# Token-layout projections of a hybrid token mixer: blocks of 512 weight columns instead of 256, with another split of the PSUM banks

## The chip, the cores and the metric

The kernel runs on one core of one Trainium2 chip. The metric is the device time of one execution in microseconds (us). The profiler's trace of one execution is read beside it. Five engines work side by side, each through its own list of instructions and strictly in that list's order: TensorE (PE, with PEld for its weight loads), VectorE (DVE), ScalarE (ACT), GpSimd (POOL) and SyncE (SP), which issues the transfers.

## The reference

Two layers work on 512 tokens: 256 context tokens and 256 latent ones, four tiles of 128 (t = 0, 1 context; t = 2, 3 latent). The width is 1024.

```
h = rms_norm(x) * (1 + scale) + shift             # scale, shift, gate from c @ w_mod
p = [h @ w for w in split(w_in)]                  # all input projections, 13872 columns
y_a = rms_norm((ssd_scan forward + backward + d*x) * silu(z))            # 16 heads of 64
s   = softmax(q k^T) for two maps of 64 dims per head                    # 8 heads
y_b = rms_norm((s_0 - lam * s_1) @ v) * silu(dz)
y_c = rms_norm((mlstm forward + backward) * sigmoid(o)) * silu(z)        # 4 heads, d_v = 256
x   = x + gate * ((sum_b sigmoid(g_b) * (y_b @ w_branch_b)) @ w_out)
```

Context tokens attend only to context, latent tokens to both. Everything is float32; the output is the latent stream after the second layer. In the second layer the context tokens are projected only where the latent ones read them (k, v, the scan inputs).

## The kernel before

**Products.** Every float32 operand of a projection is split into a high and a low part, so a product takes three matmuls per 128 rows of depth: high by high, high by low, low by high. The tokens' parts are `hh` and `hl`, the weights' parts `whi` and `wlo`.

**Weights.** They come in pieces of 128 x 1024 floats ("granules", L122ff): SP starts a transfer into `raw`, ACT casts it to `whi` (L119), DVE subtracts to get `wlo` (L82). Each of the three has three buffers.

**Two kinds of projection.** `proj_ch` (L166ff, matmuls L179 to L181) gives channels on the partitions; its moving operand is 512 tokens wide. `proj_tok` with `mm_tok` (L137 to L164, matmuls L148 to L150) gives tokens on the partitions: the token chunk is stationary, and the weights move, 256 columns at a time. Two token tiles (a "pair") share one PSUM bank, 256 columns each. q, k, v, the gates and the output projection go this way.

**PSUM.** There are eight banks, dealt out in L31 as `ACC, PE_, PM = 3, 3, 2`: three for the sums of projections (`acc`), and five for the mixers in two rotating sets (`pe`, `pm`).

**Order.** The code marks work with three bands: 0 for loads, splits and emptying of banks, 1 for the mixers, 2 for projection matmuls. A scheduler at build time puts each engine's instructions in one fixed order, with the lower band first where its operands are ready by its own model. The projections of later stages are written between the mixers' steps, so that projection matmuls stand between the mixers' matmuls on PE.

**Attention** (L899ff). For each head and query tile, the scores of the two maps go into two `pe` tiles (L917). A map has 64 dimensions; map 0 lies on partitions 0 to 63, map 1 on 64 to 127. Each map takes three matmuls, and the code writes them alternately, map 0, map 1, three times. DVE takes the row maximum (L919), ACT the exponential with its row sum (L921), DVE combines the maps in `E` (L79), PE transposes (L931, into `pe`), ACT copies (`aT`, L933), and PE multiplies with v (L935). All query tiles of a head share one `pm` bank, which ACT empties once a head (L938, L940).

**mLSTM** (L1039ff). For a head and direction, the chunks are gone through in order. In a step PE makes three products (L1067, L1072, L1088); DVE adds the state's part to the numerator (`nu`, L79), renews the state (`C`, L79), divides, and makes `kw` for the next step. The gate projections of a head (`mo_proj`, `mz_proj`) are written ahead of a `ml_core`, their use behind it.

Of the kernel before, what the change touches and what calls it, by code (L numbers as in the profile page):

```python
# [21 lines left out]
NT = 4  # L22
# [8 lines left out]
ACC, PE_, PM = 3, 3, 2  # L31
# [3 lines left out]
def hybrid_backbone_kernel(ctx: ExitStack, tc: tile.TileContext, A, out, dbg=None):  # L35
# [86 lines left out]
    def granules(srcs):  # L122

        for g in range(2):
            with band(0):
                raw = mk(wts, [P, 4, 256], "raw", bufs=3)
                c = 0
                for src in srcs:
                    n = src.shape[1]
                    nc.sync.dma_start(  # L130
                        raw[:, :, c : c + n],
                        src[g * 512 : (g + 1) * 512, :].rearrange("(k p) n -> p k n", p=P),
                    )
                    c += n
                hi = mk(wts, [P, 4, 256], "whi", F32R, bufs=3)
                lo = mk(wts, [P, 4, 256], "wlo", F32R, bufs=3)
                split(raw, hi, lo)  # L137
            yield 4 * g, hi, lo
# [12 lines left out]

    def proj_tok(srcs, lhs, pairs, evac):

        ps = {}
        with band(2):
            for p in pairs:
                ps[p] = pacc()
        for k0, hi, lo in granules(srcs):
            with band(2):
                for p in pairs:  # L160
                    mm_tok(ps[p], lhs, p * 256, k0, hi, lo)
        for p in pairs:
            with band(0):
                evac(p, ps[p].rearrange("p (t n) -> p t n", t=2))  # L164
# [37 lines left out]
    def rsqrt(src, n, scale, eps, pp=P, pool_=True):  # L202
# [6 lines left out]
        xh = mk(small, [P, 32], "rs_x", bufs=2)[:pp, :n]  # L209
        it = mk(small, [P, 32], "rs_i", I32, bufs=2)[:pp, :n]  # L210
        y = mk(small, [P, 32], "rs_y", bufs=3)[:pp, :n]
        a = mk(small, [P, 32], "rs_a", bufs=2)[:pp, :n]
# [237 lines left out]
    for l in range(depth):  # L450
# [228 lines left out]
        def silu2(ps):  # L679
            th = mk(ev, [P, 2, 256], "th", bufs=3)  # L680
            S.activation(th, ps, AF.Tanh, scale=0.5)
            zz = mk(ev, [P, 2, 256], "zz", bufs=2)
            stt(zz, th, 1.0, ps, ALU.add, ALU.mult)
            return zz

# [30 lines left out]
        ssA = mk(small, [P, NT, 4], "ssA", bufs=1)  # L716
# [76 lines left out]
        def z_proj(b):  # L793
            def f(p, ps):
                zz = silu2(ps)
                with band(1):
                    y = ya(b, p)
                    tt(y, y, zz, ALU.mult)
                    sq = mk(ev, [P, 2, 256], "sq", bufs=2)
                    for i in range(2):  # L800
                        S.activation(sq[:, i, :], y[:, i, :], AF.Square, accum_out=ssA[:, 2 * p + i, b : b + 1])

            proj_tok([wcol(O_Z + 256 * b)], hT, pq, f)


        qkv = {}

        def qkv_proj(qt, parts="qkv"):
            if qt not in qkv:
                ssq = mk(small, [P, 2, NT, 4], "ssq", bufs=3)  # L810
                qkv[qt] = {}, ssq
                with band(0):
                    if last:
                        V.memset(ssq, 64.0)
            res, ssq = qkv[qt]
            for nm_ in parts:
                n = "qkv".index(nm_)
                dst = res[nm_] = mk(p8, [P, NT, 256], "p8", bufs=6)

                def f(p, ps, dst=dst, n=n):  # L820
                    o = dst[:, 2 * p : 2 * p + 2, :]
                    S.copy(o, ps)
                    if n < 2:
                        sq = mk(ev, [P, 2, 256], "sq", bufs=2)
                        S.activation(sq, ps, AF.Square)
                        V.tensor_reduce(out=ssq[:, n, 2 * p : 2 * p + 2, :], in_=sq.rearrange("p t (m e) -> p t m e", e=64), axis=AX.X, op=ALU.add)

                proj_tok([wcol((O_Q, O_K, O_V)[n] + 256 * qt)], hT, pq if n == 0 else (0, 1), f)
# [6 lines left out]
        qkv_proj(0)  # L835
# [5 lines left out]
        qkv_proj(1)  # L841
        z_proj(0)
        z_proj(1)
        z_proj(2)
        z_proj(3)
# [12 lines left out]
        def attn_prep(qt):  # L858
            res, ssq = qkv[qt]
            with band(1):  # L860
                rq = rsqrt(ssq.rearrange("p n t m -> p (n t m)"), 32, 1.0 / 64, EPS).rearrange("p (n t m) -> p n t m", n=2, m=4)
                for n, nm_ in enumerate(("q", "k")):
                    for p in pq if n == 0 else (0, 1):
                        ts_ = slice(2 * p, 2 * p + 2)
                        x2 = res[nm_][:, ts_, :]
                        x4 = x2.rearrange("p t (m e) -> p (t m) e", e=64)
                        tt(x4, x4, bc(rq[:, n, ts_, :].rearrange("p t m -> p (t m)"), 64), ALU.mult)
                        if p == 0:
                            tt(x4, x4, gctx[:, n, :].unsqueeze(1).to_broadcast([P, 8, 64]), ALU.mult, eng=G)
                        else:  # L870
# [5 lines left out]
                            x5 = x2.rearrange("p t (m e) -> p t m e", e=64)  # L876
# [6 lines left out]
        def attn_tr(qt, h):  # L883

            res = qkv[qt][0]
            with band(1):
                out = []
                for nm_, ts, f0 in (("q", tq, lo_), ("k", range(NT), 0)):
                    pt = pm()
                    for t in ts:  # L890
                        T.transpose(chunk(pt, t), res[nm_][:, t, h * P : (h + 1) * P], ident)
# [7 lines left out]
        def attn_head(qt, h):  # L899
            vt = qkv[qt][0]["v"]  # L900
            ssB, r0B = aS[qt]
            qh, ql, kh, kl = aS[qt, h]
            with band(1):
                po = pm()
                for t in tq:
# [23 lines left out]
                    pt = pe()  # L929
# [6 lines left out]
                p3 = po.rearrange("p (t e) -> p t e", e=P)  # L936
                for p in pq:
                    S.copy(yb(qt, p)[:, :, h * P : (h + 1) * P], p3[:, 2 * p : 2 * p + 2, :])  # L938
                sq = mk(ap, [P, 512], "rt", bufs=1)
                S.activation(sq[:, lo_:], po[:, lo_:], AF.Square)  # L940
                V.tensor_reduce(out=ssB[:, q_, h], in_=sq[:, lo_:].rearrange("p (t e) -> p t e", e=P), axis=AX.X, op=ALU.add)
# [12 lines left out]
        def dz_proj(b):  # L954
            def f(p, ps):
                zz = silu2(ps)
                with band(1):
                    y = yb(b, p)
                    for i in range(2):
                        for h in range(2):  # L960
                            yy = y[:, i, h * P : (h + 1) * P]
                            stt(yy, yy, riB[b][:, 2 * p + i, h : h + 1], zz[:, i, h * P : (h + 1) * P], ALU.mult, ALU.mult)

            proj_tok([wcol(O_DZ + 256 * b)], hT, pq, f)
# [405 lines left out]
```

## Time and profile before

| | us |
|---|---|
| median of 3 runs | 1708.58 (1705.42 to 1710.35) |
| the profiled execution | 1711.2 |
| its span, first to last instruction | 1709.1 |
| PE busy | 1677.3 |
| DVE busy | 1115.3 |
| ACT busy | 762.7 |
| POOL busy | 164.0 |

The busy time of PE is that of matmuls whose ends overlap; what a matmul costs is read from the distance between the starts of two that follow each other. Of the time outside of PE's busy time most lies at the start. The mean granted clock of TensorE is 0.992 of full speed.

### The profile page before, as it was taken

To read this page: it belongs to the slowest core of one execution; us is meant where nothing else is said; L and a number is where in the kernel's file an instruction comes from. 1 tells how busy PE (TensorE), PEld (TensorE's weight loads), DVE (VectorE), ACT (ScalarE), POOL (GpSimd) and SP (SyncE) were. 2 spreads that over 40 slices of the span, in tenths; PEclk is the share of its full clock that TensorE was granted. 3 is DMA by queue.
4 is the path that set the end of the run, shared out by engine and by line. 5 is a ranking of instruction groups with operands and counts; after the bars stand their busy time and mean duration, and the time that the engine had idled before them with its cause. 6 is when DMAs were issued, how large, how long until landed. Compare 5 with 4: busy or idle time off the path is not lost.

```text
span 1709.1 us, 28774 instructions
## 1 busy us (share of the span) xinstructions
PE 1677.3 (98%) x11448; PEld 1489.2 (87%) x11448; DVE 1115.3 (65%) x2183; ACT 762.7 (45%) x1501; POOL 164.0 (10%) x192
## 2 busy tenths in 40 slices
PE   5999999999999999999999999999999999999998
PEld 2787889999899999977777789988999999999998
DVE  4698887667865666623334354898877867765565
ACT  3455644554544444422223233455555555444453
POOL 0102422101100000000010002012121100000100
PEclk8999999999999999999999999999999999999999
DMA  8522122222222222353544442322242324335654
GB/s 262 128 75 62 50 63 65 73 75 63 76 63 75 64 73 64 125 178 96 182 136 131 163 129 51 108 67 75 79 131 71 101 66 130 93 111 173 179 170 146
DMA packets 191906, 180.38 MB, mean 106 GB/s; under 512 B 20606, under 2 KB 177920, under 8 KB 191772
## 3 DMA queue, kind: packets, MB, share of 16 engines
q1 hardware_dynamic: 191772, 178.54, 35.6%
q8 instruction: 90, 1.47, 0.4%
q14 instruction: 44, 0.36, 0.1%
HBM read 177.47 MB, written 1.05 MB: 104 GB/s over the span
## 4 chain that ended last, share of the span: by engine, by line
PE 91%; DVE 4%; DMA 2%; issue 1%; ACT 1%; POOL 0%; SPq 0%; DVEq 0%; ACTq 0%; POOLq 0%
PE acc L149 12%; PE acc L148 12%; PE acc L150 12%; PE acc L179 12%; PE acc L181 12%; PE acc L180 12%; PE pe L917 2%; PE pm L935 2%; DMA wm<-in_w_mod_dram 1%; PE pm L743 1%; PE pm L1088 1%; PE pm L1067 1%; PE pe L228 1%; PE pe L1072 1%; PE pm L775 1%
## 5 line engine op out<-in xcount | busy, mean ns | idle before, releaser
L82 DVE TENSOR_TENSOR wlo<-raw,whi 128x1024 fp32r<-128x1024 f32 x274 | 348.8, 1274 | 308.4 <-ACT whi L119 306.9
L149 PE MATMUL acc<-wlo,hh 128*128 128x256 f32 x1728 | 504.9, 292 | 0.0
L150 PE MATMUL acc<-whi,hl 128*128 128x256 f32 x1728 | 503.1, 291 | 0.0
L148 PE MATMUL acc<-whi,hh 128*128 128x256 f32 x1728 | 501.5, 290 | 0.0
L119 ACT CAST whi<-raw 128x1024 fp32r<-128x1024 f32 x274 | 287.8, 1051 | 383.7 <-PE acc L180 255.0
L149 PEld LDWEIGHTS acc<-wlo,hh 128*128 128x128 f32 x1728 | 330.7, 191 | 12.6 <-issue 9.3
L150 PEld LDWEIGHTS acc<-whi,hl 128*128 128x128 f32 x1728 | 330.8, 191 | 10.4 <-issue 8.4
L148 PEld LDWEIGHTS acc<-whi,hh 128*128 128x128 f32 x1728 | 330.6, 191 | 10.0 <-issue 7.6
L179 PE MATMUL acc<-hh,whi 128*128 128x512 f32 (+1 forms) x712 | 256.3, 363 | 0.0
L180 PE MATMUL acc<-hl,whi 128*128 128x512 f32 (+1 forms) x712 | 254.9, 359 | 0.1
L181 PE MATMUL acc<-hh,wlo 128*128 128x512 f32 (+1 forms) x712 | 253.5, 357 | 0.0
L179 PEld LDWEIGHTS acc<-hh,whi 128*128 128x128 f32 x712 | 134.6, 190 | 27.0 <-issue 6.4
L180 PEld LDWEIGHTS acc<-hl,whi 128*128 128x128 f32 x712 | 135.1, 190 | 19.7 <-issue 3.0
L181 PEld LDWEIGHTS acc<-hh,wlo 128*128 128x128 f32 x712 | 135.1, 190 | 19.5 <-issue 1.9
L179 PE MATMUL acc<-yh,whi 128*128 128x512 f32 (+1 forms) x384 | 128.7, 338 | 0.0
L180 PE MATMUL acc<-yl,whi 128*128 128x512 f32 (+1 forms) x384 | 128.3, 336 | 0.0
L181 PE MATMUL acc<-yh,wlo 128*128 128x512 f32 (+1 forms) x384 | 128.2, 336 | 0.0
L921 ACT ACTIVATE E<-pe,nmax 128x512 f32<-128x512 f32 (+1 forms) x96 | 58.7, 617 | 46.9 <-DVE nmax L919 46.8
L181 PEld LDWEIGHTS acc<-yh,wlo 128*128 128x128 f32 x384 | 71.9, 188 | 8.2
L180 PEld LDWEIGHTS acc<-yl,whi 128*128 128x128 f32 x384 | 72.1, 188 | 8.0
L179 PEld LDWEIGHTS acc<-yh,whi 128*128 128x128 f32 x384 | 72.0, 188 | 7.3
L919 DVE TENSOR_REDUCE nmax<-pe 128x1 f32<-128x512 f32 (+1 forms) x96 | 53.8, 595 | 20.2 <-PE pe L917 19.9
(302 smaller groups left out, 2510.7 us busy)
## 6 DMA issues: line engine op xcount, KB each, us to landing
raw<-in_w_in_dram SPq DMA_DIRECT2D x192, 512.0 KB
raw<-in_w_branch_dram SPq DMA_DIRECT2D x48, 512.0 KB
wm<-in_w_mod_dram SPq DMA_DIRECT2D x45, 512.0 KB
raw<-in_w_in_dram SPq DMA_DIRECT2D x48, 256.0 KB
raw<-in_w_out_dram SPq DMA_DIRECT2D x16, 512.0 KB
raw<-in_w_mod_dram SPq DMA_DIRECT2D x3, 512.0 KB
xin<-in_ctx_dram SPq DMA_DIRECT2D x2, 512.0 KB
xin<-in_x_dram SPq DMA_DIRECT2D x2, 512.0 KB
```

The costliest lines, as they stand in the source:

```text
L82: (eng or V).tensor_tensor(out=o, in0=a, in1=b, op=op)
L119: S.copy(hi, raw)
L148: T.matmul(o, lhsT=xh[:, k, sl], rhs=hi[:, j, :], start=(k == 0 and i == 0), stop=False)
L149: T.matmul(o, lhsT=xh[:, k, sl], rhs=lo[:, j, :], start=False, stop=False)
L150: T.matmul(o, lhsT=xl[:, k, sl], rhs=hi[:, j, :], start=False, stop=(k == KT - 1 and i == 1))
L179: T.matmul(o, lhsT=hi[:, j, cs], rhs=xh[:, k, a:b], start=(k == 0 and first), stop=False)
L180: T.matmul(o, lhsT=hi[:, j, cs], rhs=xl[:, k, a:b], start=False, stop=False)
L181: T.matmul(o, lhsT=lo[:, j, cs], rhs=xh[:, k, a:b], start=False, stop=(k == KT - 1 and final))
L917: T.matmul(es[m][0], lhsT=x[own, qs], rhs=y[own, 0:N], start=(n == 0), stop=(n == 2))
L919: V.tensor_reduce(out=ng[:, m : m + 1], in_=es[m][0], axis=AX.X, op=ALU.max, negate=True)
L921: S.activation(e_, o, AF.Exp, bias=ng[:, m : m + 1], accum_out=rs[:, m : m + 1])
L935: T.matmul(po[:, qs], lhsT=chunk(aT, kt), rhs=vt[:, kt, h * P : (h + 1) * P], start=(kt == 0), stop=(kt == nk - 1))
```

## The change

`mm_tok` now works on one token tile with 512 weight columns, each tile in a PSUM bank of its own; a granule holds two chunks of depth by 512 columns instead of four by 256. The banks become `ACC, PE_, PM = 4, 2, 2`, so a projection of four token tiles takes all `acc` banks. q and k of two heads are one block (`qk_proj`), v is projected for four heads at once (`v_proj`, three buffers of two heads' v), and the gates and the mLSTM's v go in blocks of 512 columns too. In attention the transposes go into `pm`, the product with v has a `pm` tile per query tile, and ACT copies it out and squares it (with a row sum) for each query tile. `mo_proj` multiplies into `yc` in its evacuation, so it is written behind the cores that it reads; the order of the mLSTM stage is new. The output projection is in blocks of 512 as well, with one transfer per token tile at the end.

```diff
-ACC, PE_, PM = 3, 3, 2
+ACC, PE_, PM = 4, 2, 2
...
-    def mm_tok(ps, lhs, tcol, k0, hi, lo):
+    def mm_tok(o, lhs, tcol, k0, hi, lo):
 
         xh, xl = lhs
-        for i in range(2):
-            sl = slice(tcol + i * P, tcol + (i + 1) * P)
-            o = ps[:, i * 256 : (i + 1) * 256]
-            for j in range(4):
-                k = k0 + j
-                T.matmul(o, lhsT=xh[:, k, sl], rhs=hi[:, j, :], start=(k == 0 and i == 0), stop=False)
-                T.matmul(o, lhsT=xh[:, k, sl], rhs=lo[:, j, :], start=False, stop=False)
-                T.matmul(o, lhsT=xl[:, k, sl], rhs=hi[:, j, :], start=False, stop=(k == KT - 1 and i == 1))
...
+        sl = slice(tcol, tcol + P)
+        for j in range(hi.shape[1]):
+            k = k0 + j
+            T.matmul(o, lhsT=xh[:, k, sl], rhs=hi[:, j, :], start=(k == 0), stop=False)
+            T.matmul(o, lhsT=xh[:, k, sl], rhs=lo[:, j, :], start=False, stop=False)
+            T.matmul(o, lhsT=xl[:, k, sl], rhs=hi[:, j, :], start=False, stop=(k == KT - 1))
...
+        def v_proj(g):
+            for i in range(2):
+                vs[2 * g + i] = mk(p8, [P, NT, 256], "v", bufs=3)
+
+            def f(t, ps):
+                for i in range(2):
+                    S.copy(vs[2 * g + i][:, t, :], ps[:, 256 * i : 256 * i + 256])
+
+            proj_tok([wcol(O_V + 512 * g, 512)], hT, tiles_all, f)
...
-                    pt = pe()
+                    pt = pm()
...
+                    po = pm()[:, 0:P]
                     for kt in range(nk):
-                        T.matmul(po[:, qs], lhsT=chunk(aT, kt), rhs=vt[:, kt, h * P : (h + 1) * P], start=(kt == 0), stop=(kt == nk - 1))
...
+                    S.copy(yb(qt, t // 2)[:, t % 2, h * P : (h + 1) * P], po)
+                    sq = mk(ap, [P, P], "osq", bufs=1)
+                    S.activation(sq, po, AF.Square, accum_out=ssB[:, t, h : h + 1])
...
-            0: [lambda: qkv_proj(2, "qk")],
-            1: [lambda: qkv_proj(2, "v")],
-            2: [lambda: qkv_proj(3, "qk")],
-            3: [lambda: qkv_proj(3, "v"), lambda: dz_proj(0)],
-            5: [lambda: dz_proj(1), lambda: ml_(0), lambda: ml_(1), lambda: dz_proj(2)],
+            0: [lambda: qk_proj(2)],
+            1: [lambda: v_proj(1)],
+            2: [lambda: qk_proj(3)],
+            3: [lambda: dz_proj(0)],
+            5: [lambda: ml_qk(0, mlin), lambda: ml_qk(1, mlin), lambda: ml_v(0, mlin)],
...
+        def mo_proj(g):
+            def f(t, ps):
+                th = mk(ev, [P, 512], "th", bufs=3)
+                S.activation(th, ps, AF.Tanh, scale=0.5)
+                with band(1):
+                    y = yc.tile(g, t)
+                    stt(y, th, 1.0, y, ALU.add, ALU.mult)
...
         ml_core(0)
-        mo_post(0, ths)
-        mz_post(0, zzs)
-        mls[2] = ml_proj(2)
         ml_core(1)
...
+        ml_qk(2, mp_)
+        ml_v(1, mp_)
+        ml_qk(3, mp_)
+        dz_proj(1)
+        mo_proj(0)
+        mz_proj(0)
         ml_core(2)
...
         ml_core(3)
-        mo_post(3, mo_proj(3))
-        mz_post(3, mz_proj(3))
+        mo_proj(1)
+        mz_proj(1)
```

What the new order does on PE and ACT shows at three places. A number behind a name tells tiles of one kind apart.

**PE, first layer, attention, the scores of a head** (`pe` tiles: the two maps of one query tile; L917 before, L923 after). Before, the two maps' matmuls alternate:

```order
L931 MATMUL pe_3546<-ident_61,E_3528 128x128 x2
L917 MATMUL pe_3555<-kh_3103,qh_3094 128x256
L917 MATMUL pe_3557<-kh_3103,qh_3094 128x256
L917 MATMUL pe_3555<-kh_3103,ql_3095 128x256
L917 MATMUL pe_3557<-kh_3103,ql_3095 128x256
L917 MATMUL pe_3555<-kl_3104,qh_3094 128x256
L917 MATMUL pe_3557<-kl_3104,qh_3094 128x256
L149 MATMUL acc_3236<-wlo_3294,hh_304 128x256
```

After, in a stretch of that stage:

```order
L937 MATMUL pm_2984<-ident_61,E_2966 128x128 x2
L942 MATMUL pm_2989<-v_1245,aT_2987 128x128 x2
L923 MATMUL pe_3065<-kh_2625,qh_2616 128x512
L923 MATMUL pe_3065<-kh_2625,ql_2617 128x512
L923 MATMUL pe_3065<-kl_2626,qh_2616 128x512
L937 MATMUL pm_3016<-ident_61,E_2998 128x128 x2
L923 MATMUL pe_3067<-kh_2625,qh_2616 128x512
L923 MATMUL pe_3067<-kh_2625,ql_2617 128x512
L923 MATMUL pe_3067<-kl_2626,qh_2616 128x512
L942 MATMUL pm_3021<-v_1245,aT_3019 128x128 x2
L937 MATMUL pm_3048<-ident_61,E_3030 128x128 x4
```

The three matmuls of one map now stand together, those of the other map behind them or behind a transpose, and no projection matmul (`acc`) stands between the attention's own.

**ACT at the end of the same stretch** (`acc_3121` to `acc_3124`: the four sums of `v_proj(1)`; `v_3119`, `v_3120`: its two destinations; `pm_3055`, `pm_3091`: products with v of the first two heads). After:

```order
L943 COPY yb_2551<-pm_3055 128x128
L945 ACTIVATE osq_3061,ssB_2591<-pm_3055 128x128
L939 COPY aT_3089<-pm_3084 128x512
L927 ACTIVATE E_3306,rsum_3303<-pe_3305,nmax_3304 128x256
L927 ACTIVATE E_3308,rsum_3303<-pe_3307,nmax_3304 128x256
L835 COPY v_3120<-acc_3121 128x256
L835 COPY v_3120<-acc_3122 128x256
L835 COPY v_3120<-acc_3123 128x256
L835 COPY v_3120<-acc_3124 128x256
L943 COPY yb_2551<-pm_3091 128x128
```

The second halves of all four banks are copied only here, behind the exponentials of the next head; until then no `acc` bank is free.

**PE, first layer, mLSTM** (`va,pw`, `C,uq`, `va,kw`: the three products of a step). Before:

```order
L149 MATMUL acc_7954<-wlo_7958,hh_304 128x256
L1067 MATMUL pm_7759<-va_7297,pw_7753 128x257
L1088 MATMUL pm_7771<-va_7297,kw_7769 128x257
L150 MATMUL acc_7954<-whi_7957,hl_305 128x256
L148 MATMUL acc_7954<-whi_7957,hh_304 128x256
L149 MATMUL acc_7954<-wlo_7958,hh_304 128x256
L150 MATMUL acc_7954<-whi_7957,hl_305 128x256
```

After, at the end of the stage:

```order
L1069 MATMUL pm_6178<-va_5317,pw_6172 128x257
L1090 MATMUL pm_6190<-va_5317,kw_6188 128x257
L1069 MATMUL pm_6194<-va_5317,pw_6172 128x257
L1074 MATMUL pe_6198<-C_6192,uq_5517 128x257
L1090 MATMUL pm_6209<-va_5317,kw_6207 128x257
L1069 MATMUL pm_6213<-va_5317,pw_6172 128x257
L1074 MATMUL pe_6217<-C_6211,uq_5517 128x257
L1090 MATMUL pm_6228<-va_5317,kw_6226 128x257
L1069 MATMUL pm_6232<-va_5317,pw_6172 128x257
L1074 MATMUL pe_6236<-C_6230,uq_5517 128x257
```

The steps of both directions follow each other without a projection matmul between them.

## Rows read from the trace of the kernel before

**Rows 1.** The page: busy time of each engine, share of the span, instructions.

```profile
PE 1677.3 (98%) x11448; PEld 1489.2 (87%) x11448; DVE 1115.3 (65%) x2183; ACT 762.7 (45%) x1501; POOL 164.0 (10%) x192
```

**Rows 2.** Timeline of PE, 1098.9 to 1111.35: start us, us, line, operation.

```profile
1098.93 0.28 PE L148 MATMUL acc<-whi,hh 128*128 128x256 f32 x1
...
1111.28 0.28 PE L149 MATMUL acc<-wlo,hh 128*128 128x256 f32 x1
```

**Rows 3.** Timeline of PE, 62.98 to 89.4.

```profile
63.00 0.39 PE L180 MATMUL acc<-hl,whi 128*128 128x512 f32 x1
...
89.29 0.39 PE L181 MATMUL acc<-hh,wlo 128*128 128x512 f32 x1
```

**Rows 4.** Timeline of PE, 748.9 to 759.8.

```profile
748.99 0.40 PE L179 MATMUL acc<-yh,whi 128*128 128x512 f32 x1
...
759.76 0.40 PE L181 MATMUL acc<-yh,wlo 128*128 128x512 f32 x1
```

**Rows 5.** Timeline of PE at three places of attention.

```profile
1267.87 0.50 PE L917 MATMUL pe<-kl,qh 64*128 64x512 f32 x2
1268.30 0.39 PE L148 MATMUL acc<-whi,hh 128*128 128x256 f32 x1
...
1383.32 0.49 PE L917 MATMUL pe<-kl,qh 64*128 64x512 f32 x1
1383.74 0.50 PE L179 MATMUL acc<-hh,whi 128*128 128x512 f32 x1
...
1406.51 0.60 PE L931 MATMUL pe<-ident,E 128*128 128x128 f32 x4
1407.04 0.50 PE L917 MATMUL pe<-kh,qh 64*128 64x512 f32 x2
...
1407.93 0.39 PE L149 MATMUL acc<-wlo,hh 128*128 128x256 f32 x1
```

**Rows 6.** Timeline of PE, a product with v.

```profile
1402.27 1.05 PE L935 MATMUL pm<-p,aT 128*128 128x128 f32 x8
1403.07 0.36 PE L148 MATMUL acc<-whi,hh 128*128 128x256 f32 x1
```

**Rows 7.** Groups by line and shape on ACT: count, busy us, mean ns, idle before.

```profile
L921 ACT ACTIVATE E<-pe,nmax 128x512 f32<-128x512 f32 x64 | 43.7, 689 | 37.9 <-DVE nmax L919 37.9
L921 ACT ACTIVATION_READ_ACCUMULATOR E<-pe,nmax 128x1 f32 x96 | 19.1, 199 | 0.0
L933 ACT COPY aT<-pe 128x512 f32<-128x512 f32 x32 | 18.7, 586 | 15.8 <-PE pe L931 15.8
L921 ACT ACTIVATE E<-pe,nmax 128x256 f32<-128x256 f32 x32 | 15.0, 473 | 9.0 <-DVE nmax L919 8.9
L933 ACT COPY aT<-pe 128x256 f32<-128x256 f32 x16 | 6.0, 374 | 10.1 <-PE pe L931 10.0
```

**Rows 8.** Groups by line and shape on DVE.

```profile
L79 DVE SCALAR_TENSOR_TENSOR nu<-pe,mlc,nu 128x257 f32<-128x257 f32 x40 | 19.4, 484 | 22.3 <-PE pe L1072 20.1 <-ACT whi L119 2.0
L79 DVE SCALAR_TENSOR_TENSOR C<-C,mlc,pm 128x257 f32<-128x257 f32 x32 | 15.3, 477 | 1.7 <-PE pm L1088 1.7
L86 DVE TENSOR_SCALAR kw<-kT,mlc 128x128 f32<-128x128 f32 x48 | 12.8, 280 | 5.1 <-PE pm L1088 4.4 <-PE acc L150 0.3
L82 DVE TENSOR_TENSOR dn<-dn,nu 128x1 f32<-128x1 f32 x48 | 7.6, 158 | 1.2
```

**Rows 9.** Timeline, 598.2 to 603, an mLSTM step.

```profile
599.18 0.35 DVE L86 TENSOR_SCALAR yc<-nu,dn 128x256 f32<-128x256 f32 x1
...
599.98 0.59 PE L1072 MATMUL pe<-C,uq 128*128 128x257 f32 x2
...
600.41 0.60 PE L1088 MATMUL pm<-va,kw 128*128 128x257 f32 x2
```

**Rows 10.** Stretches: us, then busy us of PE, PEld, DVE, ACT, POOL, granted clock, DMA.

```profile
1124.00:1128.00 4.00, 2.49 (x14) 2.17 (x15) 3.82 (x11) 2.19 (x3) 0.00 (x0) 0.85 0.17 38
1128.00:1132.00 4.00, 4.00 (x16) 3.02 (x15) 3.84 (x18) 0.00 (x0) 0.00 (x0) 0.50 0.43 119
```

More of the change, by code (lines that the diff above doesn't have):

```diff
@@ L152, in proj_tok @@
-    def proj_tok(srcs, lhs, pairs, evac):
+        sl = slice(tcol, tcol + P)
[4 more added lines that the diff above has]
+            T.matmul(o, lhsT=xl[:, k, sl], rhs=hi[:, j, :], start=False, stop=(k == KT - 1))
+    def proj_tok(srcs, lhs, tiles, evac, off=0):
         ps = {}
         with band(2):
-            for p in pairs:
-                ps[p] = pacc()
-        for k0, hi, lo in granules(srcs):
+            for t, c in tiles:
+                ps[t] = pacc()
+        for k0, hi, lo in granules(srcs, 2):
@@ L159, in proj_tok @@
             with band(2):
-                for p in pairs:
-                    mm_tok(ps[p], lhs, p * 256, k0, hi, lo)
-        for p in pairs:
+                for t, c in tiles:
+                    mm_tok(ps[t][:, c:], lhs, t * P - off, k0, hi[:, :, c:], lo[:, :, c:])
+        for t, c in tiles:
             with band(0):
-                evac(p, ps[p].rearrange("p (t n) -> p t n", t=2))
+                evac(t, ps[t])
     def proj_ch(srcs, lhs, ranges, evac, halves=False, gr=None):
@@ L806, in hybrid_backbone_kernel @@
         qkv = {}
[L808 to L811, printed above, removed]
-                with band(0):
[L813 to L828, printed above, removed]
+        vs = {}
@@ new lines, in qk_proj @@
+        def qk_proj(qt):
+            ssq = mk(small, [P, NT, 2, 4], "ssq", bufs=3)
+            qk = mk(p8, [P, NT, 512], "qk", bufs=2)
+            qkv[qt] = qk, ssq
+            if last:
+                with band(0):
+                    V.memset(ssq, 64.0)
+            def f(t, ps):
+                c = 0 if t >= t0 else 256
+                S.copy(qk[:, t, c:], ps[:, c:])
+                sq = mk(ev, [P, 512], "sq", bufs=2)
+                S.activation(sq[:, c:], ps[:, c:], AF.Square)
+                V.tensor_reduce(
+                    out=ssq[:, t].rearrange("p n m -> p (n m)")[:, c // 64 :], in_=sq[:, c:].rearrange("p (m e) -> p m e", e=64), axis=AX.X, op=ALU.add
+                )
+            tiles = [(t, 0 if t >= t0 else 256) for t in range(NT)]
+            proj_tok([wcol(O_Q + 256 * qt), wcol(O_K + 256 * qt)], hT, tiles, f)
@@ L834, in hybrid_backbone_kernel @@
         ssd_core(0)
-        qkv_proj(0)
+        v_proj(0)
+        qk_proj(0)
         XT[1] = mk(sp, [P, NT, 512], "XT", bufs=2)
@@ L933, in attn_head @@
                     S.copy(aT[:, 0:N], pt[:, 0:N])
+                    po = pm()[:, 0:P]
                     for kt in range(nk):
-                        T.matmul(po[:, qs], lhsT=chunk(aT, kt), rhs=vt[:, kt, h * P : (h + 1) * P], start=(kt == 0), stop=(kt == nk - 1))
[L936 to L941, printed above, removed]
+                        T.matmul(po, lhsT=chunk(aT, kt), rhs=vt[:, kt, h * P : (h + 1) * P], start=(kt == 0), stop=(kt == nk - 1))
+                    S.copy(yb(qt, t // 2)[:, t % 2, h * P : (h + 1) * P], po)
+                    sq = mk(ap, [P, P], "osq", bufs=1)
+                    S.activation(sq, po, AF.Square, accum_out=ssB[:, t, h : h + 1])
         def attn_fin(qt):
```

217 lines of the change are left out of this document (87 added, 130 removed).

## The prediction

> **What bounds the kernel now.** I read the page's busy times first. PE is busy 1677.3 of 1709.1 us, DVE 65%, ACT 45% [rows 1]: PE is the bound, and the 32 us in which it does nothing lie mostly at the start. So two questions decide: how much time the new order gives PE to work, and whether PE still finds work while it waits for the other engines. For the first I read PE's timeline at places where one kind of matmul runs without a break; for the second the groups on ACT and DVE, and the new order.
>
> **Part 1: wider matmuls, a gain.** By the two orders, 7,104 of the projections' 256-column matmuls become 1,536, and 1,944 of 512 columns become 4,728: 2,784 times two matmuls turn into one. The price is the distance between starts. From 1098.93 to 1111.28 lie 103 distances of 256-column matmuls [rows 2]: 0.1199 us. From 63.00 to 89.29 lie 116 of 512 columns [rows 3]: 0.2266 us. From 748.99 to 759.76 lie 47 more of 512 [rows 4]: 0.2291 us. One 512 for two 256 saves 0.2398 - 0.2266 = 0.0132 us by the first, 0.0107 by the second; 2,784 of them save 37 or 30 us. The projections changed here run between mixer steps, not in a long stream, and the first matmul behind a mixer's is dearer: the first of 512 columns behind a score lasts 0.50 us (start 1383.74) [rows 5], one in a stream 0.39 [rows 3]. I take 30, with 24 and 37 as ends.
>
> The Trainium skill has another price: "TensorE: Matmul & The Clock Gate", section "Wait — 56ns, not 53.3ns?", says that a warm matmul costs its columns plus a fixed 2.5 ns or so. By that alone 2,784 fewer matmuls would save an estimated 7 us, and the sum below would end 23 us higher. The rows show 13 ns a pair [rows 2, 3], not 2.5, so I go by the rows.
>
> **Part 2: the scores lose their pairs, a loss.** A map's scores use 64 of PE's 128 rows. Two matmuls of different maps that follow each other start together: one pair of 512 columns takes 0.43 us from its start to the next matmul's (1267.87 to 1268.30), one single map's matmul 0.42 (1383.32 to 1383.74), and six in turn take 0.89 (1407.04 to 1407.93) [rows 5]. So a place in the row is worth 0.23 us, each block of scores 0.20 more for entry and exit, and the second map rides free if it alternates with the first. A 256-column place I put at 0.12 [rows 2]. Before, nearly all score sets alternate: the 288 matmuls stand in 55 blocks and take 97 places of 512 columns and 48 of 256; 11.0 + 22.3 + 5.8 = 39 us. After, `pe` has two tiles instead of three, the second map's tile comes free later than the first's, and the order puts the three matmuls of one map first: the same 288 stand in 78 blocks and take 144 and 71 places; 15.6 + 33.1 + 8.5 = 57 us. That is 18 us more. It would be 14 if the last map's matmuls could run beside earlier ones of the first map wherever both stand in one block (132 and 61 places); no row before shows such a block. About 3 of the 18 fall into the bare stretch of part 3, where they are counted with the wait; 15 remain on PE's path (11 to 16).
>
> The Trainium skill's "TensorEngine Tiling (Array Packing)", section "Key Properties", says that such row tiles work independently and that a change of tiling drains the engine. By the first rule the lower count of places would hold, some 3 us less; the second agrees with the 0.20 us per block in the rows.
>
> **Part 3: places without projection matmuls, a loss.** Before, PE's mixer steps have projection matmuls between them, so that an exponential or a state update on another engine costs PE nothing. After, `v_proj(1)` and the gates hold all four `acc` banks until their evacuations, and these wait for mixers' results. By the order there are six such places.
>
> - First layer, attention, from the first score behind `v_proj(1)` to the first `acc` matmul of `qk_proj(3)`. The second half of v waits for a v buffer, which the last product with v of the second head frees. PE's own work here: 40 passes of products with v at 0.10 (0.80 for 8) [rows 6], 28 transposes at 0.13 (0.53 for 4 from 1406.51) [rows 5], scores of seven tiles, alternating, 4 x 0.56 + 3 x 0.89: together 12.6 us, and 15.7 with the pairs lost. ACT has eight exponentials of 256 and four of 512, each with a read of its sum: 8 x 0.672 + 4 x 0.888 = 8.9; five copies of transposes, 3 x 0.586 + 2 x 0.374 = 2.5; two casts of that size, 1.2; five pairs of copy and square of 128 columns, each at most 0.95 (the 256-column copy twice, with a sum read) and taken as 0.7, 3.5; one copy of v, 0.37 [rows 7]. That is 16.5 us of ACT, and some 4 in which it waits for the first scores and maxima and the last product. So the stretch is 20.5 long, 8 more than the paired work of PE. If nothing overlaps it is 32 (+20); if all does, 15.7 (+3).
> - First layer, end of the mLSTM: both directions of `ml_core(3)` follow without `acc` matmuls, since the fourth tile of `mo_proj(1)` waits for a `th` buffer, which the first `y` of a finished core frees. A step takes PE three products of 0.43 (599.98 to 600.41) [rows 9], 1.3 us, and DVE 0.484 + 0.477 + 0.280 + 0.35 + four small ones of 0.158 = 2.2 [rows 8, 9]. Eight steps wait 8 x 0.9 = 7; with the heads of two passes, where exponentials and masks come before the first product (about two steps' waits each), 11 (4 to 18).
> - First layer, last pass of `ml_core(1)`, for the fourth tile of `mo_proj(0)`: three steps and a head, 5 (1 to 9).
> - Second layer: a short bare stretch in attention (2), one in the last mLSTM pass (1), and at the layer's entry 2.4 us less of projection matmuls beside the serial norms and gates: 5 (0 to 8).
>
> Together 29 us (8 to 55, though the ends hardly fall together; 15 to 45 is what I use).
>
> **Part 4: the clock.** Where PE is thin for a while, its granted clock falls: from 1124 to 1128 it was busy 2.49 of 4 us, and the next 4 us, full of work, ran at 0.50, the lower of its two levels, 1.2 instead of 2.4 GHz [rows 10]. Such a stretch costs 2 us. The three long places have PE at 60 to 78% by the numbers above. I count two or three falls, 5 us (0 to 15).
>
> **Part 5: the rest** I cost at nothing. The bytes and the count of weight pieces stay, with casts and subtractions off PE's path (ACT 45%, DVE 65% [rows 1]). The copies and squares of attention for each query tile are ACT's and count in part 3 only: 48 pairs of at most 0.95 are 46 us, against over 900 us in which ACT is idle. One transfer per output tile instead of several smaller ones stands at the very end and may give or take 1 us.
>
> **The sum.** 1711.2 (the profiled execution) - 30 + 15 + 29 + 5 = 1730.2. That execution is 2.6 above the median of the runs, so 1727.6, or 1728 for the median.
>
> **Rivals.**
>
> - *No change.* The bare stretches cost only half, since ACT's and DVE's queues run ahead of what I lined up, and the clock stays: 1711.2 - 30 + 15 + 14 - 2.6 = 1708. For it: ACT and DVE have much idle time [rows 1]. Against it: in these stretches they are in one chain with PE.
> - *Faster.* The mechanism is the overlap in the bare stretches: PE's longer, serial scores fill the time in which ACT works, so that waits fall to 10, and the stream price holds (37); the pairs then cost 12, the clock nothing: 1711.2 - 37 + 12 + 10 - 2.6 = 1694. It decides where waits are under some 20 us. Against it: the chain through two `pe` tiles cannot run ahead by more than one tile.
> - *Slower by the clock.* At half clock a step's three products take 2.6 us, longer than DVE's 2.2, and the attention stretch becomes PE's again at up to 31 us instead of 20.5. With 10 for attention, 4 for the mLSTM's end and 5 for the falls elsewhere, 14 above part 4's count: 1728 + 14 = 1742. For it: rows 10.
> - *The fixed price.* The gain is 7 us: 1728 + 23 = 1751. Rows 2 to 4 speak against it, and only the mixed places could bear it out.
>
> **How the numbers follow.** Forecast 0.47 (own range 1716 to 1739), no change 0.17, faster 0.16, clock 0.17, fixed price 0.03. A measurement of this kernel tells about 0.3%, 5 us, from no change: faster is below 1703.5, slower above 1713.7. Faster: 0.16 and a fifth of "no change", 0.19. Within: half of "no change" and some of the forecast's low side, 0.12. Slower: 0.69. The range of 1698 to 1747 leaves out most of "faster"'s lower half, the fixed price and the far side of the clock, some 0.2.
>
> **What would show it.** Part 1: streams of 512-column matmuls at 0.227 to 0.229, and PE's busy time in `acc` lines down by some 30 us. Part 2: the score line (L923) with single matmuls, `x1` or `x3` of one map, where before pairs start together, and blocks of 1.4 to 1.6 us for six of 512 columns. Part 3: PE idle or thin for about 20 us in the first layer's attention with ACT as the releaser, and at the end of the first layer's mLSTM with DVE as the releaser. Part 4: a lower granted clock than 0.992. The forecast is wrong if PE's idle time outside of the start stays below 15 us, or if score matmuls of one map run beside those of the other in spite of the order.

## The result and the profile after

The changed kernel takes 1736.28 us (median of 4 runs, 1734.45 to 1737.39); the kernel before took 1707.61 beside it (4 runs). The ratio is 1.0157, with a 95% interval of 1.0139 to 1.0176: slower, by 29 us. Forecast were 1728, with 1698 to 1747 as the range. The profiled execution took 1736.89 us, 25.7 more than that of the kernel before; its span is 1734.7.

The page's busy times answer to [rows 1]:

```profile
PE 1679.8 (97%) x8648; PEld 1351.3 (78%) x8664; DVE 1094.6 (63%) x2171; ACT 774.6 (45%) x1605; POOL 173.1 (10%) x188
```

PE has 2,800 matmuls fewer and is as busy as before. Where its time went is read by the distance from each matmul's start to the next one's, summed by kind over the trace from 48 us on; of a distance over 0.9 us what is above 0.6 counts as a wait:

| kind | before | after | difference | forecast |
|---|---|---|---|---|
| projection matmuls, without waits | 1360.5 | 1330.5 | -30.0 | -30 |
| scores, with their waits | 39.1 | 61.0 | +21.9 | +18, of it 3 counted in part 3 |
| the rest: other mixer matmuls and all other waits | 256.5 | 290.1 | +33.6 | +31: 29 less the 3 of the row above, and 5 for the clock |

The rows below answer to [rows 2 to 5]. First a stream of 512-column matmuls in token layout (PE's timeline: start, duration): 0.23 us from start to start.

```profile
375.10 0.39 PE L148 MATMUL acc<-whi,hl 128*128 128x512 f32 x1
375.33 0.39 PE L146 MATMUL acc<-whi,hh 128*128 128x512 f32 x1
375.56 0.39 PE L147 MATMUL acc<-wlo,hh 128*128 128x512 f32 x1
```

Then the scores of one query tile in the first layer, from the same view:

```profile
399.17 0.49 PE L923 MATMUL pe<-kh,qh 64*128 64x512 f32 x1
399.50 0.39 PE L923 MATMUL pe<-kh,ql 64*128 64x512 f32 x1
399.74 0.39 PE L923 MATMUL pe<-kl,qh 64*128 64x512 f32 x1
400.06 0.50 PE L147 MATMUL acc<-wlo,hh 128*128 128x512 f32 x1
...
401.42 0.49 PE L923 MATMUL pe<-kh,qh 64*128 64x512 f32 x1
401.76 0.39 PE L923 MATMUL pe<-kh,ql 64*128 64x512 f32 x1
401.99 0.39 PE L923 MATMUL pe<-kl,qh 64*128 64x512 f32 x1
402.32 0.50 PE L146 MATMUL acc<-whi,hh 128*128 128x512 f32 x1
```

Where before six matmuls of two maps took 0.89 us together [rows 5], here each map alone takes that: 399.17 to 400.06, and 401.42 to 402.32. The marks are `x1` instead of `x2`, and projection matmuls stand between the maps.

The stretches of part 3, as busy times in windows (us, then PE, PEld, DVE, ACT, POOL, granted clock, DMA share and GB/s):

```profile
318.00:324.00 6.00, 2.91 (x18) 1.90 (x17) 4.36 (x7) 3.53 (x7) 1.43 (x2) 0.92 0.18 62
1282.00:1292.00 10.00, 3.95 (x19) 2.78 (x18) 6.94 (x12) 2.76 (x6) 5.22 (x7) 0.85 0.37 105
355.73:373.84 18.11, 16.80 (x112) 12.47 (x111) 13.62 (x39) 14.91 (x54) 0.00 (x0) 1.00 0.10 30
639.74:645.10 5.36, 4.73 (x21) 3.13 (x19) 3.79 (x14) 2.04 (x5) 0.00 (x0) 1.00 0.00 0
699.79:717.41 17.62, 13.06 (x52) 8.91 (x51) 12.00 (x48) 7.29 (x21) 0.00 (x0) 0.90 0.00 0
1558.30:1568.90 10.60, 6.07 (x32) 4.17 (x30) 9.14 (x33) 3.95 (x11) 0.00 (x0) 1.00 0.27 91
```

In the first layer's attention the stretch without projection matmuls runs from 355.73 to 373.84, 18.1 us. ACT is busy for 14.9 us of it, but PE for 16.8: PE is idle for only 1.3 us. The mLSTM's end, 699.79 to 717.41, is 17.6 us long, with PE idle for 4.6. In the last pass of `ml_core(1)`, 639.74 to 645.10, PE is idle for 0.6. Three windows were not forecast at their size: 318 to 324 and 1282 to 1292, the beginnings of attention in the two layers, where PE's transposes wait for the normalised q and k (3 and 6 us idle), and 1558.3 to 1568.9, the end of the second layer's mLSTM (4.5 idle).

### The profile page after: what moved, and what is told of

Its sections match the earlier page's. It is cut to its first block, busy times and chain, and to the rows that moved or that the text cites. A ratio compares the mean times of both kernels' runs of the same rounds, so it can differ in the third digit from the quotient of the medians.

```text
span 1734.7 us, 23316 instructions
## 1 busy us (share of the span) xinstructions
PE 1679.8 (97%) x8648; PEld 1351.3 (78%) x8664; DVE 1094.6 (63%) x2171; ACT 774.6 (45%) x1605; POOL 173.1 (10%) x188
## 4 chain that ended last, share of the span: by engine, by line
PE 62%; DVE 4%; ACT 1%; issue 0%; POOL 0%; DVEq 0%; ACTq 0%; POOLq 0%
PE acc L177 10%; PE acc L178 10%; PE acc L179 10%; PE acc L146 7%; PE acc L147 7%; PE acc L148 7%; PE pm L1069 1%; PE pm L1090 1%; PE pe L1074 1%; PE pe L226 1%; PE pe L923 1%; PE pm L942 1%; PE pm L744 1%; DVE qk L82 1%; PE pe L1177 0%
## 5 line engine op out<-in xcount | busy, mean ns | idle before, releaser
L82 DVE TENSOR_TENSOR wlo<-raw,whi 128x1024 fp32r<-128x1024 f32 x274 | 342.8, 1252 | 330.3 <-ACT whi L119 320.5
L147 PE MATMUL acc<-wlo,hh 128*128 128x512 f32 (+1 forms) x896 | 359.0, 401 | 0.0
L146 PE MATMUL acc<-whi,hh 128*128 128x512 f32 (+1 forms) x896 | 353.1, 399 | 1.6 <-ACT sq L821 0.9
L148 PE MATMUL acc<-whi,hl 128*128 128x512 f32 (+1 forms) x896 | 352.7, 395 | 0.0
L146 PEld LDWEIGHTS acc<-whi,hh 128*128 128x128 f32 x896 | 169.4, 189 | 43.4 <-issue 7.9
L147 PEld LDWEIGHTS acc<-wlo,hh 128*128 128x128 f32 x896 | 169.7, 189 | 39.5 <-issue 8.8
L148 PEld LDWEIGHTS acc<-whi,hl 128*128 128x128 f32 x896 | 169.5, 189 | 37.2 <-issue 6.1
```

Of the source, the lines that this page charges most:

```text
L82: (eng or V).tensor_tensor(out=o, in0=a, in1=b, op=op)
```

## The experiments

Twelve kernels ran. Each median stands beside the runs of the kernel before on the same chip; ratios are to those, with their 95% interval. The time of the scores is a view of its own below: the busy time of the score line from 60 to 1700 us (us, PE busy with its count, clock, DMA, GB/s). It reads 42.84 in the kernel before and 60.94 in the changed one.

**1. The kernel before with the maps one after the other.**

```diff
-                    for n, (x, y) in enumerate(((qh, kh), (ql, kh), (qh, kl))):
-                        for m in range(2):
+                    for m in range(2):
+                        for n, (x, y) in enumerate(((qh, kh), (ql, kh), (qh, kl))):
```

> The kernel before, with the loop over the maps outside of the loop over the three products, so that the order puts a map's three score matmuls together (79 places of 256 columns and 156 of 512 in 53 blocks, before 48 and 97 in 55). Nothing else moves. Theory (pairs of maps run side by side on PE only if they alternate): the score matmuls take 56 to 64 us instead of 39, and since PE is the bound the median rises by 17 to 26 us, to 1725 to 1734. Rival (the longer scores fall into time in which PE would wait or is refilled from elsewhere): within 5 us of 1708.

Measured: 1708.18, ratio 0.9993 (0.9983 to 1.0004). My theory falls. The score line and one query tile's scores:

```profile
60.00:1700.00 1640.00, 42.39 (x288) 1.00 0.33 101
```

```profile
296.10 0.50 PE L917 MATMUL pe<-kh,qh 64*128 64x512 f32 x2
296.43 0.39 PE L917 MATMUL pe<-kh,ql 64*128 64x512 f32 x2
296.66 0.39 PE L917 MATMUL pe<-kl,qh 64*128 64x512 f32 x2
```

In PE's list the three matmuls of map 0 stand ahead of those of map 1, and yet they start in pairs (`x2`). So PE does not start them strictly in its list's order, as the section on the chip has it for every engine: the first of map 1 starts with the first of map 0, ahead of two that stand before it. The order within a block does not matter: if the other map's bank is free and its matmuls stand next in the list, they run beside the first map's. What costs is other matmuls between the maps, or a second bank that comes late. The changed kernel has the second case too, with map 0 ahead of map 1 in one block:

```profile
1329.29 0.49 PE L923 MATMUL pe<-kh,qh 64*128 64x512 f32 x1
1329.62 0.39 PE L923 MATMUL pe<-kh,ql 64*128 64x512 f32 x1
1329.86 0.39 PE L923 MATMUL pe<-kl,qh 64*128 64x512 f32 x1
1329.96 0.49 PE L923 MATMUL pe<-kh,qh 64*128 64x512 f32 x1
...
1329.13 0.68 ACT L927 ACTIVATE E<-pe,nmax 128x512 f32<-128x512 f32 x1
1329.70 0.20 ACT L927 ACTIVATION_READ_ACCUMULATOR E<-pe,nmax 128x1 f32 x1
```

The second map starts 0.67 us after the first and hardly overlaps: the exponential that frees its bank, with the read of its sum (the last two rows), ends only at 1329.90. By the corrected rule (per block, the longer map's matmuls) the orders give 39.0, 53.3 and 38.4 us for before, after and this kernel; the traces have 39.1, 61.0 and 38.8. Of the 8 us above the rule in the changed kernel, 3.4 are waits behind scores, 2.2 lie in three sets whose second bank came late (at 358, 367 and 1329 us), and 1.0 in two sets at the lower clock (322, 1292).

**2. The changed kernel with the six scores as one unit.**

```diff
+                    with tc.tile_critical():
                         for n, (x, y) in enumerate(((qh, kh), (ql, kh), (qh, kl))):
```

> The changed kernel, with the six score matmuls of a query tile issued as one unit, so that the maps alternate again (48 places of 256 and 96 of 512 in 48 blocks, against 71 and 144 in 78). The price: the first map's matmul waits for both tiles of the pe set, and by the order a second stretch without projection matmuls, with 10 us of PE's work, appears at the end of the first layer's attention. Theory: the score lines fall from 61 to 39 us, of which the new stretch eats 2 to 10: 1716 to 1726. Rival (the bare stretches are the whole loss, and the lost pairs lie in them): 1731 to 1741.

Measured: 1777.54, ratio 1.0404 (1.0383 to 1.0425), 41 us above the changed kernel, outside of both expectations. The score line falls to 44.81 us, but the unit has a price of its own, which neither theory had:

```profile
333.13 0.39 PE L146 MATMUL acc<-whi,hh 128*128 128x512 f32 x1
333.95 0.39 PE L924 MATMUL pe<-kh,qh 64*128 64x256 f32 x2 [0.43 <-issue]
...
334.82 0.41 PE L938 MATMUL pm<-ident,E 128*128 128x128 f32 x2 [0.24 <-issue]
```

From the matmul ahead to the first score lie 0.82 us instead of some 0.3, 0.43 of them idle, and behind the last one PE sits idle for 0.24 more. Over all 48 units PE is idle for 35 us ahead of the first score (never for less than 0.43) and for 7 behind the last: 42 us, as much as the loss, though some of these waits other work would have caused too. So this run does not tell the theories apart; run 9 does it in another way.

**3. The changed kernel with four buffers for the output gate's tanh.**

```diff
-                th = mk(ev, [P, 512], "th", bufs=3)
+                th = mk(mp_, [P, 512], "tho", bufs=4)
```

> The changed kernel, with four buffers of their own for the tanh of the mLSTM's output gate, so that the fourth token tile's bank is emptied without waiting for a finished core. By the order the first layer's bare stretch at the end of the mLSTM has 26 instead of 30 matmuls (6.3 us of PE's work instead of 9.7), the one of three steps before it moves. Theory (part 3, mLSTM): 4 to 10 us less, 1726 to 1732. Rival (the stage is as long as DVE's chain of steps, wherever the projections stand): within 3 us of 1736.

Measured: 1751.5, ratio 1.025 (1.0234 to 1.0265), 15 us slower than the changed kernel: both expectations fail. Projection matmuls that stood behind the mLSTM now run inside it, and what comes after it has none left:

```profile
738.99 1.04 PE L1177 MATMUL pm<-ident,y 128*128 128x128 f32 x8
739.86 1.04 PE L1177 MATMUL pe<-ident,y 128*128 128x128 f32 x8
746.08 1.12 PE L177 MATMUL acc<-yh,whi 128*128 128x512 f32 x2 [5.18 <-ACT yh L91]
```

In the changed kernel the transposes of `y` have projection matmuls between them. The wait moved to the next serial place and grew. How the 15 us are shared among this place, the lower mean clock (0.984 against 0.989) and the second layer stays open.

**4. The changed kernel with half-width matmuls.**

```diff
-            T.matmul(o, lhsT=xh[:, k, sl], rhs=hi[:, j, :], start=(k == 0), stop=False)
...
+            n = hi.shape[2]
+            for c in range(0, n, 256):
+                e = c + 256
+                T.matmul(o[:, c:e], lhsT=xh[:, k, sl], rhs=hi[:, j, c:e], start=(k == 0 and c == 0), stop=False)
...
```

> The changed kernel, with each projection matmul of 512 weight columns in token layout issued as two of 256 into the same bank. Its order differs more than that: the scheduler counts more time for the halves, and no stretch of over 3 us of mixer work stands without projection matmuls any more; the scores lose more of their pairs (88 and 167 places in 99 blocks). Theory: the projections cost 30 us more in the trace, the scores 8 to 14 more, and 17 to 27 us of waits and thin work go: 1751 to 1760. Rival (a 512 saves only a fixed few ns over two 256): the projections cost 7 us more, 1727 to 1737.

Measured: 1752.75, ratio 1.0254 (1.0239 to 1.027), inside the theory's range. The projections take 1370.6 us, 40 more than in the changed kernel: 14 ns for each of 2,784 pairs. The score line reads 74.89. PE's waits (what lies above 0.3 us of each distance over 0.75 us between matmul starts, from 65 us on) are 9 us here, 25 in the changed kernel and 8 in the kernel before. The fixed few ns are refuted. The sum comes out with two terms beyond the theory's: the projections cost 40, not 30, and all that is neither projection nor score falls by 30, not by 17 to 27.

**5 and 6. The kernel before with other bank splits.**

```diff
-ACC, PE_, PM = 3, 3, 2
+ACC, PE_, PM = 3, 2, 3      # run 5;  4, 2, 2 in run 6
```

> The kernel before with ACC, PE_, PM = 3, 2, 3: one bank less for the pe set, one more for pm; blocks of 256 as before. By the order most query tiles' scores now stand as three matmuls of one map, a projection matmul or a transpose, and three of the other: 98 blocks (55 before), of them 87 of three. Theory as the first experiments left it (two maps run side by side when both stand in one block, in whatever order, and not when other matmuls stand between them): 73 us of scores instead of 39, and two stretches without projection matmuls at the end of the first layer's attention (6 and 11 us of PE's work): 1738 to 1756. Rival (the two-tile pe set costs only the waits for its second tile, PE's list is otherwise as full as before): 1708 to 1722.

> The kernel before with ACC, PE_, PM = 4, 2, 2, the changed kernel's split, and blocks of 256 as before. By the order 100 blocks of scores, 75 us; stretches without projection matmuls of 9, 11 and 4 us of PE's work in the first layer, 6 and 5 in the second. Theory: as the split 3, 2, 3, since the pe set decides: 1740 to 1760, so that the changed kernel's 512-column blocks win back some 10 to 20 us of what the split costs. Rival (the fourth acc bank makes up for the pe tile): 1705 to 1725.

Measured: 1802.98, ratio 1.0547 (1.0523 to 1.0571), and 1811.54, ratio 1.0594 (1.057 to 1.0618). Both rivals fall, and the theory is too small by half: one `pe` bank less costs 93 us, and 102 where the bank goes to `acc`. The score line of run 5 and its attention's end:

```profile
60.00:1700.00 1640.00, 83.35 (x288) 0.98 0.30 92
```

```profile
549.32 0.49 PE L917 MATMUL pe<-kh,qh 64*128 64x512 f32 x1
549.66 0.39 PE L917 MATMUL pe<-kh,ql 64*128 64x512 f32 x1
549.89 0.39 PE L917 MATMUL pe<-kl,qh 64*128 64x512 f32 x1
553.46 0.63 PE L931 MATMUL pe<-ident,E 128*128 128x128 f32 x4 [3.18 <-DVE E L79]
```

The scores account for 40 of it. The transposes also live in `pe` there: a transpose of the last tile needs a bank, and the scores of the next one wait behind it, so PE stands still for DVE's `E`, six times and 11.4 us in all, up to 3.18 at a time. The mean granted clock falls to 0.982, from 0.992 in the kernel before, which is up to 19 us. The rest of the 93 was not traced to a place.

**7 and 8. Four buffers for v, with a control.**

```diff
-                raw = mk(wts, [P, kk, 1024 // kk], "raw", bufs=3)
+                raw = mk(wts, [P, kk, 1024 // kk], "raw", bufs=2)      # runs 7 and 8, all uses of raw
...
-                vs[2 * g + i] = mk(p8, [P, NT, 256], "v", bufs=3)
+                vs[2 * g + i] = mk(p8, [P, NT, 256], "v", bufs=4)      # run 8
```

> The changed kernel with two instead of three buffers for the incoming weights, the control for the next run; the order on PE is the same in all but a few places. Both theories: 1733 to 1742, since the weights come in well ahead.

> The same with four buffers for v instead of three (the room is that of the third weight buffer). By the order the first layer's bare stretch of 14 us of PE's work goes (4 are left, further on), but at the end of the attention one of 12 takes the place of one of 4; the scores lose 2 to 3 us of their time. Theory A (the stage has just so many projection matmuls, and what no longer waits in the middle waits at the end): within 4 us of the control. Theory B (part 3 of the prediction: the stretch costs 8 us by the v buffer alone): 6 to 12 us under the control.

Measured: 1743.3 (ratio 1.0204, 1.018 to 1.0229) and 1739.68 (1.0173, 1.0152 to 1.0193). The control is 1 us above its expectation; the third buffer for the incoming weights is worth some 7 us. The fourth v buffer brings 3.6 us, inside theory A's 4; the intervals of the ratios overlap, but each run with it (1739.88 at most) was shorter than each of the control (1743.14 at least). The score line falls by 2.8 us, from 61.13 to 58.36, which is most of it. The buffer that part 3 named held up one place; the wait went to the next.

**9. Pairs by a wait.** The first score of a tile waits for the second map's exponential of the tile before.

```diff
+                            if last_exp and m == 0 and n == 0:
+                                tc.add_manual_dep(mm.ins, last_exp[-1], mybir.DependencyInfo(mybir.DependencyClass.Sync, mybir.DependencyReason.DATA), reason="pair")
...
+                        last_exp.append(S.activation(e_, o, AF.Exp, bias=ng[:, m : m + 1], accum_out=rs[:, m : m + 1]).ins.name)
```

> The changed kernel, where the first map's first score matmul of a query tile also waits for the exponential of the second map of the tile before, so that both maps' pe tiles are free at once. By the order the scores stand in 66 blocks, 34 of them with all six; by the rule of side-by-side maps 42 us, against 61 measured. The price is a first map that starts up to one exponential (0.9 us) later; the order shows a stretch of 6 us of PE's work more at attention's end. Theory (lost pairs are about 18 us of the loss, on PE's path): 1717 to 1727. Rival (the later start costs what the pairs bring, or the lost pairs lie in waits): 1732 to 1742.

Measured: 1726.26, ratio 1.0101 (1.0082 to 1.012), 10 us under the changed kernel, as the theory has it. The score line:

```profile
60.00:1700.00 1640.00, 47.73 (x288) 0.99 0.32 100
```

It lost 13 us, and 10 of them reach the end.

**10. Pairs and four buffers for v**, `sq` and `zz` with one buffer each for the room.

```diff
-                vs[2 * g + i] = mk(p8, [P, NT, 256], "v", bufs=3)
+                vs[2 * g + i] = mk(p8, [P, NT, 256], "v", bufs=4)
```

> As the run before, with four buffers of v besides (the room comes from sq and zz, one buffer each). By the order the bare stretch of 13 us of PE's work in the first layer's attention is split into pieces of 3 to 4, with one of 7.5 at the end; scores 40 us. Theory: 3 to 10 us less than the run before, 1710 to 1722. Rival (waits only move to the end of the stage, and the single buffers of sq and zz add some): within 3 us of it or slower.

Measured: 1721.29, ratio 1.0062 (1.0038 to 1.0087), 5 us less than run 9, as the theory has it, though the two intervals overlap a little. The reason is another than the theory's: PE's waits, counted as for run 4, are 25 us here and 27 there, so they moved, while the score line falls from 47.73 to 44.95.

**11. The kernel before with 3, 2, 3 and the transposes in pm.**

```diff
-ACC, PE_, PM = 3, 3, 2
+ACC, PE_, PM = 3, 2, 3
...
-                    pt = pe()
+                    pt = pm()
```

> The kernel before with 3, 2, 3 banks again, but with the attention's transposes in pm, where the changed kernel has them. By the order the scores still stand in 97 blocks (69 us instead of 39), but the stretches of 6 and 11 us without projection matmuls are gone. Theory (two things make the two-tile pe set dear: the lost pairs, some 30 us, and the transposes that queue for the same two tiles, the other 60): 1738 to 1752. Rival (the transposes' home hardly counts, it is all in the scores): 1785 to 1805.

Measured: 1750.9, ratio 1.0243 (1.0222 to 1.0263): the theory. The transposes' home is worth 52 of run 5's 93 us. The 41 us that remain are the scores' (75.77 on the score line, 33 more than before) and some waits.

**12. Pairs by a wait, and half-width matmuls** (the diffs of runs 4 and 9 together).

> Both edits together: the first map waits for the second map's bank (as in the run with pairs), and each 512-column projection matmul in token layout is issued as two of 256. By the order the scores take 41 us (60 blocks), and no stretch of over 3 us of mixer work stands without projection matmuls from the first layer's attention on. Theory (the terms add: the run with halves alone, 1753, less its 27 us of lost pairs): 1722 to 1732, about the same as pairs with whole blocks, so that the wide matmuls' 30 to 40 us only pay for the waits that come with them. Rival (halves and pairs together leave PE as full as in the kernel before): 1705 to 1715.

Measured: 1715.7, ratio 1.0037 (1.0023 to 1.0052): just outside the rival's range, 6 us under the theory's. The two stages of the first layer, attention and mLSTM, from the first score to the first transpose of `y`:

```profile
304.20:507.10 202.90, 202.45 (x1559) 182.41 (x1558) 157.73 (x387) 118.28 (x334) 18.81 (x16) 1.00 0.21 64
507.10:677.90 170.80, 170.80 (x1205) 160.64 (x1204) 107.10 (x315) 71.51 (x155) 2.51 (x5) 1.00 0.23 70
```

PE is full and at full clock. In the changed kernel the same two stages have it idle for 4 and 7 us:

```profile
318.80:546.40 227.60, 223.21 (x1117) 171.03 (x1116) 153.81 (x377) 121.59 (x328) 17.39 (x14) 0.99 0.21 59
546.40:727.70 181.30, 174.08 (x783) 141.58 (x789) 106.70 (x317) 72.44 (x167) 2.50 (x5) 0.99 0.23 65
```

Against run 9, which differs from it in the width alone, the projections cost 35.9 us more (13 ns a pair), and the run is still 10.6 us faster by the medians. So with the pairs kept, the wide matmuls lose more by the order that comes with them than they win; without the pairs it is the other way, run 4 is 16 us slower than the changed kernel. Run 12 is the fastest of the changed kernel's variants, and 0.4% slower than the kernel before; none of them beats it.

## Why the prediction was right

The direction holds, the time is within 8 us of the forecast, and each term has about its size: the table has -30.0 + 21.9 + 33.6 = 25.5 us, the forecast -30 + 18 + 31 = 19. Inside of the terms several reasons do not hold.

- **Part 1** is right: 30.0 for 30, 11 ns a pair. That it is right to the microsecond is luck, since the same 2,784 pairs are worth 40 and 36 us in runs 4 and 12, 14 and 13 ns each. The price that the prediction set aside is that of the Trainium skill, "TensorE: Matmul & The Clock Gate", section "Wait — 56ns, not 53.3ns?": a fixed 2.5 ns or so per matmul. None of these runs bears it out.
- **Part 2** has the size (21.9 for 18) and the wrong reason for a part of it. "The second map rides free if it alternates with the first" is more than is needed: run 1 shows that it rides free in any order within a block. So the prediction's last sign of being wrong did come: in the changed kernel, too, 13 blocks hold both maps and do not alternate throughout, and ten of them took no longer than one map alone. Here is one of them, with the matmul behind it, 0.88 us from start to start for six of 512 columns:

```profile
360.56 0.50 PE L923 MATMUL pe<-kh,qh 64*128 64x512 f32 x2
...
361.44 0.66 PE L898 MATMUL pm<-ident,qk 128*128 128x128 f32 x4
```

  Counted by this rule, the lost pairs are 14 us, 4 less than forecast (the prediction says "some 3"). The other 8 are waits behind scores, late second banks and the lower clock, as said for run 1, and those I had not priced; that they fill the gap is luck. What the traces bear out is the rule that the prediction put beside its own, from the Trainium skill's "TensorEngine Tiling (Array Packing)", section "Key Properties", that row tiles work independently. Runs 9 and 11 show that the term is on PE's path: 13 us of scores back are 10 us of time, 33 more are most of 41.
- **Parts 3 and 4** have nearly the sum (33.6 for 31) and not the places. Of the 33.6 some 17 us lie in the mLSTM's matmuls (14 in the first layer, where 11 + 5 were forecast), 10 in attention's other than scores, the rest elsewhere. The attention stretch was 18.1 us long (20.5 forecast), but PE was not thin in it: it was idle for 1.3 us in all, nearly all of them behind ACT. So that sign of part 3, PE idle or thin for about 20 us, failed. The mLSTM's end was 17.6 long (some 21 by the prediction's figures, eight steps of 1.3 and 11 of waits), with PE idle for 4.6. There the steps don't wait for DVE by 0.9 us each: PE waits at the heads of the passes, and the steps follow at PE's own pace, for a while at the lower clock (1.07 us for a product instead of 0.60, with a granted clock of 0.90 over the window shown above):

```profile
703.97 0.70 PE L1069 MATMUL pm<-va,pw 128*128 128x257 f32 x2 [1.58 <-DVE pw L82]
...
706.89 1.07 PE L1090 MATMUL pm<-va,kw 128*128 128x257 f32 x2
...
710.41 0.70 PE L1074 MATMUL pe<-C,uq 128*128 128x257 f32 x2 [0.23 <-DVE C L79]
...
713.52 0.70 PE L1069 MATMUL pm<-va,pw 128*128 128x257 f32 x2 [1.96 <-DVE pw L82]
```

  The last pass of `ml_core(1)`, priced at 5, has PE idle for 0.6. What I put too low are the starts of attention, about 9 us idle in the two windows shown, where I had 2 for the second layer and nothing for the first, and the end of the second layer's mLSTM, 4.5 idle for 1. In all PE is idle for 26 us from 65 us on, 8 in the kernel before. That places priced too high and too low make up the forecast's sum is luck.
- **The named causes of part 3 are not the whole cause.** The v buffer and the tanh buffers do hold the banks where the order says so, but runs 3 and 8 show that without them the wait goes elsewhere. Run 12 keeps both and the four banks, and has no such stretch. What leaves PE bare is the order as a whole: how much projection work is left when the serial places come. In the changed kernel the first score starts 37 us later (319.12 against 281.93), with that much more of other work ahead of it. Why the scheduler spreads the halves better was not tried and stays open. Weights that come late are not the cause: PE waits for a cast (`whi`) only once, 2.9 us at 57.76, ahead of all the places named here.
- **The clock** cost about what was forecast: the mean granted clock went from 0.992 to 0.989, (1 - 0.989) x 1734.7 - (1 - 0.992) x 1709.1 = 5.4 us, or less where PE had to wait anyhow. The lower level shows behind four of the places where PE had been idle: after 323, 705, 1289 and 1569 us. The last of them, right behind the end of the second layer's mLSTM:

```profile
1569.00:1572.00 3.00, 3.00 (x14) 3.00 (x15) 1.53 (x4) 2.52 (x11) 0.71 (x2) 0.50 0.03 5
```

- **What makes the kernel slower**: 22 us of scores and 34 of waits and lower clock stand against 30 won. The runs point to the third `pe` bank, given up for the fourth `acc` bank, and to the order. In the kernel before, the bank costs 93 us by itself (run 5); the transposes in `pm` take back 52 (run 11), and the wide matmuls give 30. That leaves 11 of the 29 us; the other 18 come with the new order, and no run shows them by themselves. Two `pe` tiles need not cost this much: run 12 has them, keeps the pairs by its wait, and is 7 us slower than the kernel before.

## What to carry to other kernels

Price a change of tile width with the PSUM banks that it takes from others: 11 ns on each of 2,784 matmul pairs, 30 us, were won, and a rotating set that went from three banks to two lost more (41 in run 11). Count on an unrolled, statically ordered engine how much filler each serial stage has left; a buffer added at one place moves the wait unless filler is added too. And when two instructions are to run side by side, see that they stand next to each other with both outputs free, in whichever order.

## What the runs showed of the hardware that I had not expected

- Two score matmuls on different halves of PE's rows start within 10 ns of each other even when two more of the first half stand between them in the list (run 1: the score line takes 42.39 us, against 42.84 where they alternate).
- Six matmuls issued as one unit leave PE idle for 0.43 us or more ahead of each of 48 units, where the changed kernel has no idle time ahead of any of its 78 blocks of scores, and for 7 us in all behind them (run 2).
